# An embedding lookup with position add: instruction streams and semaphores written by hand, stores in four interleaved transfers

## The chip, the cores and the metric

The kernel runs on one core of a Trainium2 chip. The metric is the device time of one execution in microseconds (us); of the kernel before, 10 runs gave a median of 184.74 us (184.63 to 184.87). The profile is of one further execution.

A core has five engines that run their own instruction streams[...]: PE (TensorE), DVE (VectorE), ACT (ScalarE), POOL (GpSimd) and SP (SyncE). Transfers between the chip's memory (HBM) and the on-chip memory (SBUF, 128 partitions) are made by 16 DMA engines, which SP and POOL feed by two different queues.

## The reference

```python
batch, seq_len, vocab_size, d_model = 32, 512, 50000, 512
# indices (32, 512) int32; embedding_table (50000, 512) float32; position_embed (512, 512) float32
token_embed = embedding_table[indices]
return (token_embed + position_embed).astype(np.float32)
```

For each of 32 x 512 tokens a row of 2 KB is fetched from the table, the row of its position is added, and the sum is written: 33.5 MB are read at scattered places and 33.5 MB are written.

## The kernel before

A sequence of 512 tokens is laid over 128 partitions with K = 4 tokens in each, so that partition p holds tokens 4p to 4p + 3; a sequence is a tile of 128 x 4 x 512 floats, 8 KB in a partition, 1 MB in all. One *gather* (an indirect DMA, line 88, issued from POOL) fetches column k of a sequence, one row for each partition, 256 KB. One *add* on DVE (line 94) adds the position rows of that column in place. A *store* (line 97, issued from SP) writes one, two or four columns to `out`.

Ahead of the loop over the 32 sequences SP loads the indices of the first sequence (`idx0`, line 49), all indices with a sequence in each partition (`idx_raw`, line 51) and the position rows (`pos_sb`, line 56). As a gather wants its indices one to a partition, `idx_raw` is turned: DVE converts it to float (line 68), PE transposes it in four steps against an identity that POOL made (lines 60 to 73), and DVE converts it back (line 75). ACT copies the position rows to PSUM (line 79), from where DVE adds them. The first sequence needs only `idx0`, so its gathers start before the turning is done.

The kernel is written for a framework that takes care of buffers and semaphores: it gives each tile a buffer of a pool (`data_pool`, BUFS = 20), puts the needed waits before each instruction, and has the engines run in the order of the source. Each gather and each store is counted by one of eight semaphores in turn; thus a gather also waits for the gather eight before it, and a store for the store eight before it. What one instruction cannot wait for by itself is put into wait-only instructions (EVENT_SEMAPHORE) in front of it. At the end SP waits for all these semaphores in ten such instructions (they carry the line of the launch, L132), and the engines meet in a barrier.

How a sequence is cut into stores is set by hand (lines 100 to 106): sequences 0, 1 and 31 in four stores of one column each (256 KB, 2 KB to a partition), sequences 2 to 5 and 30 in two stores of two columns (512 KB, 4 KB to a partition), all others in one store of 1 MB (8 KB to a partition). That makes 12 + 10 + 24 = 46 stores. Every store or part of a sequence has a buffer of its own.

## Time and profile before

| what | value |
|---|---|
| median of 10 runs | 184.74 us |
| the profiled execution's own time | 184.82 us |
| its span, from the first to the last instruction of the profile | 183.1 us |
| what lies around the span | 1.72 us |
| bytes moved | 68.33 MB, mean 373 GB/s |
| gathers: count, mean time of one on POOL | 128, 0.949 us |
| adds: count, mean time of one on DVE | 128, 0.688 us |
| stores: count, time of one on SP | 46, 0.332 us |
| first gather starts, last gather starts | 2.78 us, 162.12 us |
| last add ends | 172.43 us |
| last store issued | 173.88 us |
| last DMA packet ends | 174.35 us |

How to read it: the page gives each engine's busy time, and below it the span in 40 slices of 4.58 us with the busy tenths of each. The line DMA is the mean busy share of the 16 DMA engines. A group of instructions stands under its line of the kernel, with its operation, the tile that it writes and reads, and how often it occurs. An SPq row is an instruction that SP's queue carries out; it counts as no busy time. In the table by stage each row has the stretch, its length, the busy time and count of the five engines, the clock, the share of DMA and the GB/s. The packet records of the trace have the time, the size and the queue of each single packet: q0 carries the gathers, q1 what SP issues.

Lines 121 and 132 are lines of the launch: the start and the end that the framework puts around the kernel.

### The profile page before, as it was taken

The numbers are of one execution on the slowest core, as the hardware profiler recorded it, in microseconds if no ns is written. First come the engines' busy times: TensorE is split into PE (matmuls) and PEld (weight loads), VectorE is DVE, ScalarE is ACT, GpSimd is POOL, SyncE is SP. The second block draws the span as 40 slices with busy tenths as digits, with TensorE's granted clock in tenths as the row PEclk, the third lists the DMA queues.
The fourth block names the chain that finished last, engine by engine and source line by source line (L and its number), as shares of the span: only waits on it lengthen the run. The fifth ranks groups of instructions, "written<-read, shape, count | busy, mean of one in ns | idle before, by whom it ended". The sixth has DMA issues, their size and how long they took to land.

```text
span 183.1 us, 480 instructions
## 1 busy us (share of the span) xinstructions
PE 0.7 (0%) x4; PEld 0.6 (0%) x4; DVE 87.6 (48%) x130; ACT 3.6 (2%) x5; POOL 122.1 (67%) x134
## 2 busy tenths in 40 slices
PE   0000000000000000000000000000000000000000
PEld 0000000000000000000000000000000000000000
DVE  1253654555647444448255554544547464643300
ACT  3400000000000000000000000000000000000000
POOL 4777777777777777877877877777777777740000
DMA  4889999999999999999999999999999999999900
GB/s 137 311 248 375 388 397 375 407 384 408 392 402 412 411 398 419 405 419 401 414 409 413 418 413 417 406 424 408 414 418 415 422 409 419 408 415 417 372 6 0
DMA packets 17635, 68.33 MB, mean 373 GB/s; under 512 B 3008, under 2 KB 3008, under 8 KB 14560
## 3 DMA queue, kind: packets, MB, share of 16 engines
q0 software_dynamic: 10240, 33.56, 48.2%
q1 hardware_dynamic: 7392, 34.74, 46.3%
q14 instruction: 3, 0.02, 0.0%
HBM read 34.74 MB, written 33.55 MB: 373 GB/s over the span
## 4 chain that ended last, share of the span: by engine, by line
issue 58%; DMA 18%; POOL 8%; SPq 5%; DVE 3%; DVEq 1%; POOLq 1%
DMA data<-in_embedding_table_dram,idx_t 10%; POOL data L88 8%; DMA out_dram<-data 7%; SPq L97 5%; DVE data L94 3%; DMA idx<-in_indices_dram 1%; DVEq L94 1%; POOLq L88 1%
## 5 line engine op out<-in xcount | busy, mean ns | idle before, releaser
L88 POOL DMA_INDIRECT data<-in_embedding_table_dram,idx_t x124 | 117.6, 948 | 37.8 <-issue 37.2
L94 DVE TENSOR_TENSOR data<-data,pos_ps 128x512 f32<-128x512 f32 x128 | 86.7, 688 | 80.4 <-DMA data<-in_embedding_table_dram,idx_t 41.2
L88 POOL DMA_INDIRECT data<-in_embedding_table_dram,idx x4 | 4.0, 996 | 2.5 <-DMA idx<-in_indices_dram 1.6
L79 ACT COPY pos_ps<-pos_sb 128x512 f32<-128x512 f32 x4 | 2.4, 589 | 5.0 <-DMA pos_sb<-in_position_embed_dram 3.3
L68 DVE CAST idx_f<-idx_raw 32x512 f32<-32x512 int32 x1 | 0.6, 606 | 3.5 <-DMA idx_raw<-in_indices_dram 3.5
L79 ACT ACT_TABLE_LOAD x1 | 1.3, 1283 | 0.8 <-PEq L121 0.8
L75 DVE CAST idx_t<-turned 128x128 int32<-128x128 f32 x1 | 0.3, 292 | 0.8 <-PE turned L73 0.8
L73 PE MATMUL turned<-ident,idx_f 32*128 32x32 f32 x4 | 0.7, 301 | 4.3 <-DVE idx_f L68 4.3
L73 PEld LDWEIGHTS turned<-ident,idx_f 32*128 32x128 f32 x4 | 0.6, 208 | 4.2 <-issue 4.2
L121 POOL MEMSET const-float32-0.0<- 128x1 f32 x1 | 0.1, 104 | 0.3 <-issue 0.3
L60 POOL MEMSET ones<- 32x32 f32 x1 | 0.1, 115 | 0.3 <-POOLq L121 0.3
L62 POOL TENSOR_SCALAR_AFFINE_SELECT ident<-ones 32x32 f32<-32x32 f32 x1 | 0.2, 204 | 0.1
L121 POOL MEMSET const-uint8-127<- 128x1 uint8 x1 | 0.1, 121 | 0.0
L121 POOL MEMSET const-bfloat16-1.0<- 128x1 bf16 x1 | 0.1, 115 | 0.0
L121 POOL MEMSET const-float32-1.0<- 128x1 f32 x1 | 0.1, 107 | 0.0
## 6 DMA issues: line engine op xcount, KB each, us to landing
out_dram<-data SPq DMA_DIRECT2D x24, 1024.0 KB
out_dram<-data SPq DMA_DIRECT2D x10, 512.0 KB
out_dram<-data SPq DMA_DIRECT2D x12, 256.0 KB
data<-in_embedding_table_dram,idx_t POOLq DMA_INDIRECT x124
pos_sb<-in_position_embed_dram SPq DMA_DIRECT2D x4, 256.0 KB
idx_raw<-in_indices_dram SPq DMA_DIRECT2D x1, 128.0 KB
data<-in_embedding_table_dram,idx POOLq DMA_INDIRECT x4
idx<-in_indices_dram SPq DMA_DIRECT2D x1, 4.0 KB
```

Source lines behind the costliest of these rows:

```text
L60: nc.gpsimd.memset(ones[:], 1.0)
L62: nc.gpsimd.affine_select(out=ident[:], in_=ones[:], pattern=[[-1, B]], compare_op=mybir.AluOpType.is_equal, fill=0.0, base=0, channel_mul ...
L68: nc.vector.tensor_copy(out=idx_f[:].rearrange("b p k -> b (p k)"), in_=idx_raw[:, :, 0])
L73: nc.tensor.transpose(turned[:, k, :], idx_f[:, :, k], ident[:])
L75: nc.vector.tensor_copy(out=idx_t[:], in_=turned[:])
L79: nc.scalar.copy(out=pos_ps[k][:], in_=pos_sb[k][:])
L88: nc.gpsimd.indirect_dma_start(out=data[:, j, :], out_offset=None, in_=table, in_offset=bass.IndirectOffsetOnAxis(ap=where, axis=0),)
L94: nc.vector.tensor_tensor(out=data[:, j, :], in0=data[:, j, :], in1=pos_ps[k][:], op=add)
L97: nc.sync.dma_start(out=out_rows[b][:, at : at + n, :], in_=data[:])
L121: nc = _bacc.Bacc("TRN2", target_bir_lowering=False, num_devices=1)
```

## The change

The tiles are kept, and so are the loads, the turning of the indices, the gathers and the adds. What is new:

```diff
-    data_pool = ctx.enter_context(tc.tile_pool(name="data", bufs=BUFS))
+    slots = [sbuf(f"slot{n}", [P, K, D], f32) for n in range(SLOTS)]
...
+    stores = []
+    for b in range(B):
+        if b == 0 or b == B - 1:
+            split, combs = (1, 1, 1, 1), 1
+        elif b <= 2:
+            split, combs = (2, 2), 2
+        else:
+            split, combs = (K,), COMBS
+        at = 0
+        for n in split:
+            for j in range(combs):
+                adds = min(b * K + at + n + j, B * K)
+                stores.append((adds, b, at, n, j, combs))
+            at += n
+    stores.sort()
...
+    def rounds(g):
+        return 16 * (g // LANES + 1)
+
+    with tc.tile_critical():
...
+        nc.gpsimd.wait_ge(s_first, 16)
+        for g in range(B * K):
+            b, k = divmod(g, K)
+            if g == K:
+                nc.gpsimd.wait_ge(s_idx, 1)
+            if b >= SLOTS and k == 0:
+                done = sum(1 for x in stores if x[1] == b - SLOTS)
+                nc.gpsimd.wait_ge(s_out[b - SLOTS], 16 * done)
+            where = idx0[:, 2 * k : 2 * k + 1] if b == 0 else idx_t[:, k, b : b + 1]
+            ins = nc.gpsimd.indirect_dma_start(
+                out=slots[b % SLOTS][:, k, :],
...
+            ).then_inc(s_gather[g % LANES], 16)
+            if g >= LANES:
+                ins._wait_ge(s_gather[g % LANES], rounds(g - LANES))
...
+        for g in range(B * K):
+            b, k = divmod(g, K)
+            if b == 0:
+                nc.vector.wait_ge(s_ps, k + 1)
+            part = slots[b % SLOTS][:, k, :]
+            nc.vector.tensor_tensor(
+                out=part, in0=part, in1=pos_ps[k][:], op=add
+            )._wait_ge(s_gather[g % LANES], rounds(g)).then_inc(s_add, 1)
...
+        for adds, b, at, n, j, combs in stores:
+            done = s_out.get(b, s_rest)
+            rest += done is s_rest
+            nc.sync.dma_start(
+                out=out_rows[b][j::combs, at : at + n, :],
+                in_=slots[b % SLOTS][j::combs, at : at + n, :],
+            )._wait_ge(s_add, adds).then_inc(done, 16)
+        nc.sync.wait_ge(s_rest, 16 * rest)
```

## The prediction

> **What bounds the kernel now.** I read the page first: busy shares, then the forty slices and the DMA queues; then the table by stage, the rows of the gather and of the SP queue, and last the two ends. The page of the kernel before:

> ```profile
> PE 0.7 (0%) x4; PEld 0.6 (0%) x4; DVE 87.6 (48%) x130; ACT 3.6 (2%) x5; POOL 122.1 (67%) x134
> ...
> DMA  4889999999999999999999999999999999999900
> ...
> q0 software_dynamic: 10240, 33.56, 48.2%
> q1 hardware_dynamic: 7392, 34.74, 46.3%
> ```

> No engine is near 100%, but the sixteen DMA engines are: the two queues' packets took 48.2% + 46.3% of the span, and the digits are 9 from the fourth slice until the last two, which are 0. The table by stage, whose last two columns are the DMA share and GB/s:

> ```profile
> 2.00:10.00 8.00, 0.66 (x4) 0.55 (x4) 2.05 (x4) 2.45 (x5) 5.70 (x6) 1.00 0.85 282
> 10.00:20.00 10.00, 0.00 (x0) 0.00 (x0) 4.56 (x8) 0.00 (x0) 7.56 (x9) 1.00 0.96 325
> 20.00:40.00 20.00, 0.00 (x0) 0.00 (x0) 10.70 (x16) 0.00 (x0) 15.12 (x17) 1.00 1.03 393
> 40.00:163.00 123.00, 0.00 (x0) 0.00 (x0) 65.50 (x97) 0.00 (x0) 93.08 (x99) 1.00 1.02 411
> 163.00:171.00 8.00, 0.00 (x0) 0.00 (x0) 3.99 (x6) 0.00 (x0) 0.07 (x1) 1.00 1.02 418
> 171.00:175.00 4.00, 0.00 (x0) 0.00 (x0) 0.83 (x2) 0.00 (x0) 0.00 (x0) 1.00 0.69 265
> 175.00:183.10 8.10, 0.00 (x0) 0.00 (x0) 0.00 (x0) 0.00 (x0) 0.00 (x0) 1.00 0.00 0
> ```

> From 20 to 171 us DMA is full. From 175 to 183.1 us nothing moves and no engine computes: 8.1 us of pure ending. The rows of the gather (L88), of the stores (L97) and of the end (L132), with minimum/median/maximum ns:

> ```profile
> L88 POOL DMA_INDIRECT data<-in_embedding_table_dram,idx_t x124: 945/949/957, 8.0 to 162.1; - x124
> ...
> L97 SPq DMA_DIRECT2D out_dram<-data x46: 332/332/700, 8.8 to 173.9; - x46
> L97 SPq EVENT_SEMAPHORE  x44: 17/17/701, 10.6 to 172.5; - x44
> ...
> L132 SPq EVENT_SEMAPHORE  x11: 2/3/699, 175.3 to 182.5; - x11
> ```

> POOL starts a gather every (162.12 - 2.78) / 127 = 1.2547 us and is never held up. A gather of 262,144 bytes and its store ask for 524,288 / 1.2547 = 418 GB/s; DMA delivers 411. So POOL and DMA are almost level, and the gathers' queue falls behind slowly: the chain of waits shows 4.01 us from issue to landing at 8 us, 7.56 us at 88 us, and the last one takes about 9 us. What is new in the last row: ten of the eleven wait-only instructions lie between the last store and 182.28 us, and their starts are 0.7 or 1.4 us apart although the semaphores they name are filled (the last packet ended at 174.35, the last store's semaphore at 174.58). A wait on SP costs 17 ns before 170 us; from 170.1 us on, SP steps in units of 0.7 us.

> [...] in the packet records 256 KB stores ran at 84 ns for 2 KB, 1 MB stores at 309 ns for 8 KB, so row length made a difference of 8%, and transfer size none that I can see. [...] 832 4-byte packets on q1 are 52 x 16. [...] the one 32-partition transfer here (the block idx_raw, loaded beside pos_sb) had a median of 237 ns for a 4 KB packet, against 159 ns elsewhere.

> **The change part by part.** The sum is made on the profiled execution: 184.82 us, span 183.1, so 1.72 us lie around it; it stands 0.08 us above the median of 184.74.

> *Start.* The critical section puts two SP instructions (a no-op and a branch) ahead of the first load, and the other engines wait for them. Such steps are some 0.05 us apart here. All that follows moves: +0.15, bounds 0 and +0.5 us.

> *POOL.* Still 128 gathers of 0.949 + 0.305 us. The look-back goes from 8 gathers (10.0 us) to 16 (20 us), the buffers from 20 to 24, one for each sequence; neither wait held POOL before, as its starts are even throughout. Gain 0. It would matter if landing came to exceed 10 us, and is now a cover of 11 us. The new waits for a slot stand before gathers 96, 100 and so on, with later gathers behind them; they are for stores about 20 sequences old. Cost 0; the cover is some 100 us.

> *DVE, ACT, PE.* The same 128 adds of 0.688 us, with one wait in each and four extra for pos_ps, which is ready as before. DVE is busy at 48%, so nothing.

> *SP issue.* 46 stores become 128, but 44 wait instructions go. 128 x (0.332 + 0.05) = 49 us, spread over 165: one issue for each 1.25 us add, at the end two for each of adds 125 to 127, 0.76 us. Hidden while SP is at its fast step; at the slow step, two records of 0.7 us, a store would take 1.4 us and no longer keep up with an add.

> *DMA work.* 82 more stores x 9 ns for one increment packet in each engine = +0.74 us. 1 MB goes from 2 KB to 8 KB packets: 128 x (4 x 84 - 309) / 16 = -0.22 us; 3 MB from 4 KB: 384 x (2 x 159 - 309) / 16 = -0.22 us. Sum +0.30 us, all on the path, as DMA is full. The packet time itself, 309 ns for 8 KB, is the unknown: finer mixing of stores and gathers could take away the gathers' excess (165.7 ns on average against 159: 6.7 x 64 packets x 128 gathers / 16 = 3.4 us)[...]. I take 309 and keep -3 and +9 for the range.

> *Order of the stores.* Quarter j of a sequence waits for j more adds, so its stores trail by up to three adds, 0.75 MB. The stores behind it in SP's queue wait for later adds anyway. Near 10 to 20 us, where the DMA share is only 0.96, this opens a hole: +0.5 (0 to +1.8, all 0.75 MB at 411 GB/s). At the end it fills one: from 171 to 175 DMA moved 265 x 4 = 1.06 MB, which at 411 takes 2.6 us, so 1.4 us stood empty around the last adds and SP's slow last issue; with half a megabyte of stores still queued I take 1.0 of it back.

> DMA then ends at 174.35 + 0.15 + 0.30 + 0.5 - 1.0 = 174.30.

> *End.* Ten wait-only instructions that check 19 semaphores become one wait for s_rest, then six short instructions and a round among the engines. Before, this took 182.29 - 174.35 = 7.94 us. At the fast step: 0.25 us until the last semaphore (174.34 to 174.58 before), 7 x 0.05, and one round of 0.4 us (two final rounds took 182.34 to 183.10), together 1.0 us. Then the final rounds and rest, 0.82 us as before. 174.30 + 1.0 + 0.82 + 1.72 = 177.84; with half of one slow step of 0.7 us on top, 178.2. At the slow step the seven cost 4.9 us, and if each leaves two records, 9.8.

> **The rivals.** *A, the end goes fast* (178.2): fewer waits, all data already landed. For it: SP ran at 17 ns for 170 us with this kind of instruction. Its doubt: I don't know why SP slows down; if it is the place in the stream (after some 95 instructions), the slow stretch falls among stores near the middle and is hidden.

> *B, the slow step stays at the end* (181.7): it starts at about 170 us whatever the instruction. Seven steps at 0.7 us instead of 0.05: +4.6 us, and the last seven stores take 1.4 us instead of 0.38, of which the DMA's rest hides most; the 1.0 us taken back at the end and part of the tail go: 178.2 + 4.6 = 182.8 with single steps throughout, less about 1.1 us since some steps pair up (the last three before ended within 0.02 us). For it: in the trace it is tied to nothing but the time and SP's own stream.

> *C, slower* (187.4): [...] 28 sequences x 4 transfers x 2 packets in each engine = 224 packets. At 350 ns instead of 309 they cost 224 x 0.041 = 9.2 us, on a path that is full: 178.2 + 9.2 = 187.4. It decides from (184.82 - 178.2) / 224 = 30 ns, thus from 339 ns on. For it: idx_raw's slow packets. Against: [...] idx_raw was a block loaded beside others.

> *D, no change*: A's gain eaten by a mild C or by B at two records for each step; a narrow window of 0.7 us.

> **How the numbers follow.** A 0.44, B 0.30, C 0.23, D 0.03. The likeliest is A, so 178.2; its own range is 176.6 to 179.8. The lower end is A with part of the 3.4 us of excess gone; the upper, 187.5, takes in B (up to 184.4) and the nearer half of C. A measurement here can tell about 0.2%, 0.37 us, from no change: faster 0.74, same 0.03, slower 0.23.

> **What would show it.** Right: no run of 0.7 us waits behind the last store, and the zero slices at the end shrink from 8.1 us to about 2; DMA near 411 GB/s between 40 and 163 us; gathers still 1.255 us apart; 8 KB packets at 309 ns. B shows as SP instructions 0.7 us apart after 170 us, C as 8 KB packets above 339 ns and fewer GB/s in the middle. The hole would show as less than 325 GB/s between 10 and 20 us. The prediction fails outright if POOL's cadence changes, or if the slow step comes so early that the stores fall behind the adds.

## The result, and the profile after

The changed kernel takes 195.95 us (195.04 to 196.51, 8 runs) against 184.73 (184.56 to 184.90, 28 runs) for the kernel before on the same chip: ratio 1.060, 95% interval 1.0588 to 1.0611. It is slower by 11.2 us, and outside the range of the prediction. The profiled execution took 196.55 us with a span of 194.8. The experiments ran on five chips, on three of which the kernel before takes 184.5 to 184.9 us and on two 178.2; so each ratio below is against the kernel before on the same chip, and times are compared only where the chip is the same or the text says otherwise.

From the page of the changed kernel:

```profile
PE 0.7 (0%) x4; PEld 0.6 (0%) x4; DVE 88.1 (45%) x130; ACT 3.6 (2%) x5; POOL 122.1 (63%) x134
...
DMA  4989999999999999999999999999999999835460
...
q0 software_dynamic: 10240, 33.56, 47.0%
q1 hardware_dynamic: 7936, 34.75, 43.7%
```

POOL and DVE did the same work as before (122.1 us, and 88.1 against 87.6). The last six digits of the DMA row, 999900 before, are now 835460. The end is no longer empty; for some 20 us, in four slices, it is about half full. The table by stage (stretch, its length, busy time and count of the five engines, clock, DMA share, GB/s):

```profile
2.00:10.00 8.00, 0.68 (x4) 0.55 (x4) 1.89 (x4) 2.63 (x5) 5.45 (x6) 1.00 0.83 271
10.00:20.00 10.00, 0.00 (x0) 0.00 (x0) 4.56 (x8) 0.00 (x0) 7.56 (x9) 1.00 0.94 318
20.00:40.00 20.00, 0.00 (x0) 0.00 (x0) 10.62 (x16) 0.00 (x0) 15.12 (x17) 1.00 1.00 369
40.00:163.00 123.00, 0.00 (x0) 0.00 (x0) 67.35 (x99) 0.00 (x0) 93.13 (x99) 1.00 1.01 398
163.00:171.00 8.00, 0.00 (x0) 0.00 (x0) 3.66 (x6) 0.00 (x0) 0.30 (x1) 1.00 0.83 342
171.00:180.00 9.00, 0.00 (x0) 0.00 (x0) 0.00 (x0) 0.00 (x0) 0.00 (x0) 1.00 0.46 189
180.00:190.00 10.00, 0.00 (x0) 0.00 (x0) 0.00 (x0) 0.00 (x0) 0.00 (x0) 1.00 0.53 211
190.00:194.80 4.80, 0.00 (x0) 0.00 (x0) 0.00 (x0) 0.00 (x0) 0.00 (x0) 1.00 0.07 25
```

The last add ends at 170.3 us, two microseconds earlier than before. After it no engine computes, yet DMA moves 189 to 211 GB/s until 190.46 us: stores that could have gone long ago. Who holds them back? The rows of the gather (L125) and of the store on SP's queue (L167) say it, with minimum/median/maximum ns; the first two lines are from the whole span, the last two are the store's row in two windows, 8 to 47 us and 52 to 184 us:

```profile
L125 POOL DMA_INDIRECT slot<-in_embedding_table_dram,idx_t x124: 945/949/959, 8.2 to 162.4; - x124
...
L167 SPq DMA_DIRECT2D out_dram<-slot x128: 3/700/1559, 9.5 to 188.8; - x128
...
L167 SPq DMA_DIRECT2D out_dram<-slot x26: 332/472/1559, 9.5 to 45.9; - x26
L167 SPq DMA_DIRECT2D out_dram<-slot x91: 5/700/1480, 52.5 to 183.0; - x91
```

The gathers are untouched. A store takes SP 0.47 us (the median) until about 46 us and 0.70 us from 51 us on, mostly with another 0.70 to 0.76 us of gap before the next: (183.0 - 52.5) / 90 = 1.45 us from store to store, while the adds that release them come every 1.255 us. This is the slow step that the kernel before showed only at its end. SP falls behind by 0.2 us for each store, and 98 stores later it is 18 us late. 262,144 bytes in 1.455 us are 180 GB/s, close to the 189 of the stretch from 171 to 180 us.

The second thing to see is behind the last store, in the rows of the critical section's own exit (L98):

```profile
L98 SPq NOP  x2: 18/18/18, 0.8 to 193.8; - x2
...
L98 POOLq DRAIN  x1: 2515/2515/2515, 191.2 to 191.2; - x1
```

SP has seen all stores at 191.0 us, then waits for POOL, whose drain takes 2.515 us, and only then executes its NOP at 193.8.

### The profile page after: what moved, and what is told of

It reads as the page before. It is cut to its first block, busy times and chain, and to the rows that moved or that the text cites. A ratio compares the mean times of both kernels' runs of the same rounds, so it can differ in the third digit from the quotient of the medians.

```text
span 194.8 us, 480 instructions
## 1 busy us (share of the span) xinstructions
PE 0.7 (0%) x4; PEld 0.6 (0%) x4; DVE 88.1 (45%) x130; ACT 3.6 (2%) x5; POOL 122.1 (63%) x134
## 3 DMA queue, kind: packets, MB, share of 16 engines
q0 software_dynamic: 10240, 33.56, 47.0%
HBM read 34.74 MB, written 33.55 MB: 351 GB/s over the span
## 4 chain that ended last, share of the span: by engine, by line
POOL 56%; issue 23%; DMA 5%; DVE 4%; SPq 0%; POOLq 0%
POOL slot L125 56%; DMA slot<-in_embedding_table_dram,idx_t 4%; DVE slot L154 4%; DMA idx<-in_indices_dram 1%; SPq L197 0%; SPq L98 0%; POOLq L123 0%
## 5 line engine op out<-in xcount | busy, mean ns | idle before, releaser
L125 POOL DMA_INDIRECT slot<-in_embedding_table_dram,idx_t x124 | 117.6, 948 | 37.8 <-issue 37.8
L154 DVE TENSOR_TENSOR slot<-slot,pos_ps 128x512 f32<-128x512 f32 x128 | 87.2, 688 | 77.6 <-issue 58.6
L125 POOL DMA_INDIRECT slot<-in_embedding_table_dram,idx x4 | 4.0, 997 | 2.5 <-DMA idx<-in_indices_dram 1.6
```

What stands on the lines that cost most here:

```text
L125: ins = nc.gpsimd.indirect_dma_start(out=slots[b % SLOTS][:, k, :], out_offset=None, in_=table, in_offset=bass.IndirectOffsetOnAxis(ap=whe ...
L154: nc.vector.tensor_tensor(out=part, in0=part, in1=pos_ps[k][:], op=add)._wait_ge(s_gather[g % LANES], rounds(g)).then_inc(s_add, 1)
```

## The experiments

The questions were four: is it SP's slow step or the shape of the stores; what brings the slow step on; what does the hand-written exit cost; and is there anything left of the hoped-for gain. "SP slow" below means instructions of 0.7 or 1.4 us, or gaps of that size with nothing to wait for.

**Shape and queue of the stores** (before: 184.51 us). The first kernel stores full sequences whole, 44 stores instead of 128:

```diff
-COMBS = 4
+COMBS = 1
```

> The changed kernel with COMBS = 1: sequences 3 to 30 each in one store of 1 MB, so 44 stores in place of 128, all else kept. Theory S (SP falls into a step of 0.7 us, a store then takes 1.455 us, longer than the 1.255 us between two gathers, and the stores pile up): with one store in 5 us SP's issue can't be late, DMA ends near 174 us and the whole takes 177 to 183 us, depending on whether the step reaches the end. Theory R (what costs is the new order and the hand-written waits: stores that trail the adds, waits that hold POOL or DVE): little changes, 190 us or more. Theory T (transfers of 32 partitions are slow in the DMA engines): also under 184, but then the 8 KB packets of the changed kernel would have been longer than 309 ns, and they were 311.

Measured 184.42 us, ratio 0.9993 (0.9986 to 1.0000). From the table by stage:

```profile
40.00:163.00 123.00, 0.00 (x0) 0.00 (x0) 65.29 (x97) 0.00 (x0) 92.94 (x99) 1.00 1.02 413
```

SP stays fast until all data is out (413 GB/s, last packet at 174.98), and turns slow at 176.0 us, after three fast instructions of the exit. So the hand-written streams by themselves are neither the loss nor a gain here: the slow step is back where it was before, at the end, and the time misses the 177 to 183 us that were expected.

The second keeps the 128 stores and gives every other one to ACT:

```diff
+        for i, (adds, b, at, n, j, combs) in enumerate(stores):
+            queue = nc.scalar if i % 2 else nc.sync
```

> The changed kernel with every second store issued from ACT, whose stream is idle after 6 us. Same transfers, same order, same waits. Theory S: each of the two queues has one store in 2.5 us, under the 1.455 us of the slow step, so stores keep up with the adds even if both slow down: 177 to 184 us. Theories R and T: the transfers and their order are the same, so 194 to 197 us as in the changed kernel.

188.40 us, ratio 1.0231 (1.0191 to 1.0270). The rows of the stores:

```profile
L168 SPq DMA_DIRECT2D out_dram<-slot x64: 332/468/577, 9.2 to 171.1; - x64
L168 ACTq DMA_DIRECT2D out_dram<-slot x64: 339/476/548, 10.3 to 172.6; - x64
```

The stores keep up (413 GB/s; SP has seen all of them land at 175.34 us, at 191.0 in the changed kernel), neither engine is slow before the end, and SP is slow from 176.05 to 187.26 us, all through the exit. That exit is why the time lies above the expected 177 to 184 us. The third keeps one store for each add, but as a column of all 128 partitions (2 KB rows), and not as a *comb*, a store that takes every fourth partition:

```diff
-        if b == 0 or b == B - 1:
-            split, combs = (1, 1, 1, 1), 1
...
+        split, combs = (1, 1, 1, 1), 1
```

> The changed kernel with all 32 sequences cut by columns, 128 partitions and 2 KB in each, four stores for a sequence, so again 128 stores of 256 KB and one for each add, but none waits for a later add and none takes every fourth partition. Theory S: the number of SP's instructions is the same, so SP slows down and the stores pile up: 192 to 200 us; the 2 KB packets add 28 x 128 x (4 x 84 - 309) / 16 = 6 us to the DMA work where that is the limit. Theories R (trailing) and T (32 partitions): fast, 178 to 186 us.

186.99 us, ratio 1.0120 (1.0100 to 1.0139). The store's row between 56 and 180 us:

```profile
L162 SPq DMA_DIRECT2D out_dram<-slot x89: 5/700/1395, 55.5 to 178.7; - x89
```

SP is slow here too, from 54 us on; so it isn't the comb. But a store costs (178.7 - 55.5) / 88 = 1.40 us instead of 1.45, and the last one goes at 181.5 instead of 188.8. So 195.95 - 186.99, about 9 of the 11 us lost, come with the comb (two chips, on which the kernel before differs by 0.2 us), and not by its packets (311 ns for 8 KB, as before; their median is 309 in both). Where they come from is in part an estimate: under the slow step a store costs 0.05 us more, which makes some 5 us for 98 of them, and the combs start further behind the adds (30 stores were out at 51.1 us, here 34 at 51.4), which makes another 4 times 1.4 us. The time is below the expected 192 to 200 us for the same two reasons. The fourth is the 44-store version with three wait-only instructions ahead of each 1 MB store, for a semaphore filled long before (six waits in the source; the build puts two into one instruction):

```diff
+            if combs == 1 and n == K:
+                for _ in range(6):
+                    nc.sync.wait_ge(s_first, 16)
```

> The kernel of whole stores (COMBS = 1) with three instructions ahead of each 1 MB store that only wait for a semaphore filled at the start: SP has as many instructions as the changed kernel, but 44 stores. If the slow step comes from the number of instructions that SP has carried out (theory S1), SP slows down in the middle; as four instructions of up to 1.4 us fit into the 5 us of a sequence only just, the time is 182 to 192 us. If it comes from the number or kind of the DMAs it issues (theory S2), the waits take 17 ns and the time is that of the kernel of whole stores within 0.5 us.

187.25 us, ratio 1.0138 (1.0121 to 1.0154). The fillers' row, before and after 30 us:

```profile
L169 SPq EVENT_SEMAPHORE  x5: 28/28/176, 25.1 to 29.6; - x5
L169 SPq EVENT_SEMAPHORE  x79: 5/700/1397, 30.3 to 175.9; - x79
```

With 44 stores, but four SP instructions for each sequence, the slow step is there from 30.3 us. What counts is the number of SP's instructions, not the number of its DMAs.

**Stores from ACT** (another chip; before: 178.16 us, and in the four traces SP shows no slow step). The first two replace `nc.sync.dma_start` of the store by `nc.scalar.dma_start` in the 44-store version and in the changed kernel, the third does the same in the kernel before, and the fourth is the changed kernel with two combs for four:

```diff
-COMBS = 4
+COMBS = 2
```

> The kernel of whole stores (COMBS = 1) with all 44 stores issued from ACT; SP keeps the six loads and the end. Theory S2 (the slow step belongs to SP and grows out of the work that SP has done): SP has done almost nothing, so its end runs at the fast step; data done at about 175.3, then 0.3 us, 2.5 us for POOL's drain and 0.7 us of rounds, so 180 to 181 us. Theory E (the slow step is tied to the end of a run, whatever SP did): 184 to 185 us as with the stores on SP. Should ACT fall into the slow step in SP's place, it shows as ACT instructions 0.7 us apart.

> The changed kernel with all 128 stores issued from ACT in place of SP. If the slow step is SP's alone, ACT issues each store in 0.48 us and keeps up with the adds: 180 to 185 us. If any engine that issues a store in every 1.25 us falls into the step, ACT does, and the time is 194 to 197 us as in the changed kernel.

> The kernel before with its 46 stores issued from ACT, nothing else. SP then has six loads and the ten waits of the end. Theory S2: the ten waits take some 0.05 us each in place of 0.7, and the last two stores are not held up by 1.4 us: 176.5 to 178.5 us. Theory E: the end is as before, 183.5 to 185 us.

> The changed kernel with COMBS = 2: sequences 3 to 30 in two stores of every second partition, 72 stores on SP, one in 2.5 us. If the slow step comes from the number of instructions SP has carried out (about 40 in the changed kernel), SP slows down in the middle too, but a store of 1.455 us still keeps up, and the time is 182 to 186 us. If it comes from how close they follow each other, SP stays fast until the end: 182 to 185 us. The two differ in the trace: SP instructions 0.7 us apart from 60 us on, or only after 165 us.

Measured 180.68, 181.27, 177.69 and 181.85 us; ratios 1.0144 (1.0109 to 1.0179), 1.0177 (1.0139 to 1.0215), 0.9981 (0.9959 to 1.0003) and 1.0225 (1.0185 to 1.0266). The second is the changed kernel with its stores free of SP:

```profile
L167 ACTq DMA_DIRECT2D out_dram<-slot x128: 338/476/1002, 8.8 to 171.7; - x128
...
40.00:163.00 123.00, 0.00 (x0) 0.00 (x0) 66.31 (x97) 0.00 (x0) 93.14 (x99) 1.00 1.02 413
```

All stores keep up and data ends at 175.55 us, 14.9 us before that of the changed kernel. But this chip can't tell that ACT is the cure, as SP isn't slow on it either, with 72 stores of its own (median 0.472 us); that the first three times lie in the expected ranges is no test of it. What the runs do show is that the second still loses 1.8%, and the version with 72 stores on a fast SP 2.2%: without any slow step the change doesn't gain either. In all three hand-written versions POOL's drain takes 2.5 us at the exit; in the kernel before POOL drains from about 160 to 172 us, beside the last adds.

**The exit, and both kernels again** (before: 184.90 us). The changed kernel and the kernel before unaltered; then the changed kernel with one line behind POOL's last gather, so that POOL drains beside the last adds; then that line in the 44-store version with stores on ACT:

```diff
+        nc.gpsimd.drain()
```

> The changed kernel once more, unaltered, beside the kernel before. Theory S (SP's step of 0.7 us belongs to the place where the kernel runs, and costs the change time only where it comes while stores are left): if the kernel before takes about 184.6 us here, 195 to 196.5 us, SP at 1.40 to 1.46 us per store from some point on; if it takes about 178.2 us, SP steps at 0.05 us throughout, a store takes 0.48 us, stores keep up with the adds, and what is left is the exit: 181.3 us (ratio 1.015 to 1.02), with a gap of about 2.3 us ahead of SP's no-op while POOL drains. Rival (the store pattern itself brings the slow step, wherever it runs): 195 us in either case.

> The kernel before, unaltered, with a trace from the same chip as the others of this set: ratio 1.00. Theory S: if it takes about 178.2 us, no SP instruction takes 0.7 us and the ten wait-only instructions at the end are over within 0.5 us of the last store's semaphore; if about 184.6 us, they are 0.7 or 1.4 us apart as in the first profile.

> The changed kernel with one drain on POOL directly after its last gather, so that POOL's 2.5 us of draining run beside the last adds and stores and not behind the last store. Theory E (POOL's drain is serial in the exit): 2.0 to 2.4 us less than the unaltered changed kernel of the same set, and the drain at the exit takes under 0.1 us. Rival (the drain at the exit takes its 2.5 us whatever was drained before, or waits for the stores): no difference, within 0.3 us.

> Hand-written streams with the full sequences in one store of 1 MB (44 stores), all stores issued from ACT, and the drain on POOL after the last gather. Theories S and E together: nothing is left for a slow SP to hold up but the exit's handful of steps. If the kernel before takes about 178.2 us here: 180.7 - 2.3 = 178.4 us, ratio 0.995 to 1.005. If it takes about 184.6 us: stores end near 175.4, then eight or nine SP steps of 0.7 to 1.4 us, 182 to 185 us. Rival to E: 180.7 us, ratio 1.014.

196.26, 184.96, 193.74 and 184.61 us; ratios 1.0605 (1.0577 to 1.0632), 1.0001 (0.9992 to 1.0010), 1.0468 (1.0444 to 1.0492) and 0.9980 (0.9970 to 0.9991). The drain at the exit of the third:

```profile
L98 POOLq DRAIN  x1: 41/41/41, 190.6 to 190.6; - x1
```

41 ns instead of 2,515: the early drain is worth 196.26 - 193.74 = 2.5 us. The changed kernel repeats its loss on this second chip, with SP slow from 47 us on, and the kernel before its slow end. The fourth has SP idle for 171 us, and then its exit at 175.5 goes fast for three instructions and slow to 183.5 us. A long rest does not keep SP fast for the ten short instructions of an exit.

**What brings the slow step on.** For every run I counted SP's instructions and took off one for each 1.40 us that passed, never below zero; what remains is the *excess*. In the runs up to and with the second pause probe below, ten of eleven onsets after 40 us came at an excess of 3.2 to 3.9, as if SP had a *stock* of about three instructions that may come faster (the last expectation of this group has nine, which is one short). The eleventh was 7.3, at 54 us; two earlier ones, at 30 and 39.6 us, were 7.4 and 10.7. And early in a run the rule doesn't hold. These are the stores of the kernel before and their waits from 8 to 40 us:

```profile
L97 SPq DMA_DIRECT2D out_dram<-data x16: 332/332/348, 8.8 to 39.5; - x16
L97 SPq EVENT_SEMAPHORE  x15: 17/17/17, 10.6 to 39.9; - x15
```

That is one instruction per us, 1.0 against 0.714, and an excess of 6.5 to 10.6 from 13 to 49 us, without a slow step. So early on SP has more in hand than three; why is not known. (Single stores of 0.73 to 1.56 us between 20 and 36 us are not counted as the slow step: on the chip without it SP's and ACT's stores took up to 0.93 and 1.00 us there.) The rule was read off afterwards, so it had to forecast something. The probes start from the 44-store version with stores on ACT and the early drain, and let SP execute wait-only instructions that hold nobody up:

```diff
+        for g in range(B * K):
+            nc.sync.wait_ge(s_add, g + 1)
+            nc.sync.wait_ge(s_add, g + 1)
```

> The version with 44 stores on ACT and the early drain, whose SP now also executes one wait-only instruction for each add (128, 0.797 per us), which nothing waits for until the end. Theory R (SP's slow step comes once it has had more than one instruction per 1.40 us for a while, whatever they are): SP turns slow at 45 to 60 us, as with 128 stores, then takes 1.4 us per wait and is through with them at 176 to 182 us; the time grows by at most 5 us, for nothing else hangs on SP. Rival M (it needs DMA issues among SP's instructions): all waits take under 0.05 us beyond their semaphore until the last add at about 171 us. Where the kernel before takes about 178.2 us, no slow step in any case, and the run tells nothing on R.

> As the one before, but SP executes these waits only for adds 1 to 24 and 65 to 128, with a pause from about 40 to 90 us. Theory R with a stock that the pause fills: slow from some 25 to 45 waits after the pause, at 120 to 145 us. Rival T (what counts is the time: from about 50 us on, any instruction that follows within 1.4 us is slow): slow within three waits of the pause, at 90 to 95 us.

> As the first probe, but SP executes three waits for four adds: 0.60 per us, below one per 1.40 us (0.714). Theory R: never slow before the end at about 172 us. Rival T: slow from about 50 us on where two waits stand 1.25 us apart.

These three ran where the kernel before takes 178.15 us. No SP instruction was slow, so they tell nothing of the rule: 179.28, 178.93 and 179.28 us, ratios 1.0057 (1.0030 to 1.0084), 1.0044 (1.0019 to 1.0069), 1.0055 (1.0038 to 1.0072). They do show that hand-written streams with an early drain, and with the waits of the probe, still lose half a per cent there. Also the waits did not run as written: put by the build into pairs, the first one ended only at 93 us in the first probe, and then two instructions came for each add.

The next has a pause in the waits, and ran where the kernel before takes 184.88 us:

```diff
+            if g < 64 or g >= 96:
+                nc.sync.wait_ge(s_add, g + 1)
+                nc.sync.wait_ge(s_add, g + 1)
```

> As the probe with a pause, but SP executes its waits for adds 1 to 64, pauses for adds 65 to 96 (about 85 to 128 us), and goes on for adds 97 to 128; stores are on ACT. Meant for a run where the kernel before takes about 184.6 us (where it takes 178.2, it tells nothing). Theory R: slow from 45 to 60 us on, at 1.4 us per wait; after the pause fast again for at least ten waits. Rival M (it needs DMA issues on SP): fast until the end. Rival T (the time counts): fast or slow at first, slow within three waits after the pause.

187.17 us (one run). The waits (two lines, L174 and L175) again began late, at 72 us. L174 in the windows 72 to 75.5, 76 to 112, 130 to 135.6 and 135.6 to 176 us:

```profile
L174 SPq EVENT_SEMAPHORE  x2: 28/28/28, 74.2 to 75.2; - x2
L174 SPq EVENT_SEMAPHORE  x13: 5/700/1395, 76.2 to 110.5; - x13
L174 SPq EVENT_SEMAPHORE  x3: 28/28/28, 132.4 to 135.5; - x3
L174 SPq EVENT_SEMAPHORE  x14: 5/700/1387, 137.8 to 174.2; - x14
```

Wait-only instructions with no DMA of SP's own among them turn slow, so DMA issues are not needed. After the pause five waits are fast, not ten as I had expected, and then it is slow again: a small stock refills, and the time in the run doesn't decide. The last probe puts the stock's size to the test, with bursts on either side of it:

```diff
+        for b in range(8, B - 1):
+            for n in range(3 if b < 20 else 5):
+                nc.sync.nop()._wait_ge(s_add, (b + 1) * K).then_inc(s_tick, 1)
```

> The version with 44 stores on ACT and the early drain; SP executes, besides, wait-only instructions in bursts, one burst after the last add of a sequence: three for each of sequences 8 to 19, five for each of sequences 20 to 30. Theory R with its stock, as read from the runs so far (nine of eleven onsets after 40 us came when SP had executed 3.2 to 3.9 instructions more than one per 1.40 us): no slow step before sequence 20, at about 114 us; then the fourth or fifth instruction of the first burst of five takes 0.7 or 1.4 us, and so in the bursts after it. Rival Q (only a rate that lasts counts, with a stock above ten): no slow step before 160 us. Rival T (the time counts): slow from the first burst, at about 52 us. Where the kernel before takes about 178.2 us, no slow step, and the run tells nothing.

186.15 us (one run; before 184.58). The bursts' row in the windows 40 to 114, 114 to 120 and 120 to 184 us:

```profile
L174 SPq EVENT_SEMAPHORE  x36: 17/17/133, 54.3 to 111.1; - x36
L174 SPq EVENT_SEMAPHORE  x5: 17/168/709, 115.4 to 117.8; - x5
L174 SPq EVENT_SEMAPHORE  x50: 2/700/1396, 121.1 to 182.9; - x50
```

Twelve bursts of three: all fast, for 57 us. The first burst of five, from the trace (start us, took ns):

```
115.363   17
115.429   17
115.496  168
116.365  701
117.765  709
```

The fourth is slow, at an excess of 3.3, as forecast from a stock of about three. The rivals, a lasting rate alone and the time, are out for this stage of a run, as far as one run shows.

**The best version.** The kernel before with its stores on ACT, on a chip where the kernel before takes 184.58 us:

```diff
-            nc.sync.dma_start(out=out_rows[b][:, at : at + n, :], in_=data[:])
+            nc.scalar.dma_start(out=out_rows[b][:, at : at + n, :], in_=data[:])
```

> The kernel before with all its stores issued from ACT, and nothing else changed. Theory R with its stock: where the kernel before takes about 184.6 us, SP comes to its ten wait-only instructions at the end with its stock full, so three of them are fast and the other seven and the short ones after them go at 0.7 to 1.4 us: 182 to 184.5 us, ratio 0.985 to 0.999, as the last stores are no longer issued at the slow step. Rival (the end is the same, since the waits at the end take what they took): 184.6 us, ratio 1.00. Where the kernel before takes about 178.2 us: 177.7 us, ratio 0.997 to 1.000 as in the first run of this version.

183.88 us, ratio 0.9961 (0.9947 to 0.9975). SP's waits at the end start at 170.2 us, five are fast while they wait for real, and the slow step comes at 175.6, at an excess of 3.1. On the other kind of chip it was 0.9981, with an interval that takes in 1, so no gain is shown there. It lost on neither, and the change is one word.

## Why the prediction was wrong

The measured 196.55 us of the profiled execution lie 18.35 above 178.2. In the prediction's own steps:

*SP issue* is the step that failed, with 14.9 us: data ended at 190.46, and at 175.55 in the same program with the stores on ACT. These are two chips, but with every other store on ACT, on a chip with the slow step, all stores had landed by 175.34. The prediction priced it rightly: "at the slow step, two records of 0.7 us, a store would take 1.4 us and no longer keep up with an add". It then took "Hidden while SP is at its fast step" for the case. Its case A even hoped that a slow stretch "falls among stores near the middle and is hidden", although that step had shown that it can't be. What was missing is when the step comes. It was not place in the stream (instruction 96 before, 40 after, 58 and 29 in two experiments) and not the time; after the first 50 us it is rate. SP is then good for one instruction per 1.40 us, 0.714 per us, and about three on top (an excess of 3.2 to 3.9 at ten of eleven onsets). Before: two for each sequence of 5.02 us, 0.40 per us, until the smaller stores of the end, with a wait each, came 1.8 us apart (four steps from 163.88 to 171.16 us), 1.1 per us. Changed: one for each add, 0.797 per us. Both numbers stood in the prediction ("one issue for each 1.25 us add" and 1.4 us); that the first would bring on the second was not seen. Merging each wait into its store, which saved 44 instructions, could not make up for 82 stores more. The fast price was low as well: 0.332 us is that of a store of 128 partitions, one of 32 takes 0.468, which would still have been hidden.

*End* was too low by 2.2 us: 4.38 us from the last packet to the end of the span against 1.0 + 0.82 and the half step. This is the drain of POOL (2.515 us). The prediction counted SP's short instructions and "one round of 0.4 us", but not what each engine does in that round. SP's own steps were fast there, because the slow stretch had just ended.

*Order of the stores* and *DMA work*: without the slow step data ended at 175.55, not 174.30, and 1.28 us after that of the kernel before with stores on ACT (174.28, same chip). The 44-store version ended at 174.82. So hand-written streams cost 0.54 us and combs 0.73 us in the data, where the steps summed to -0.05. These are single profiles, and the runs of each version spread by 0.8 to 1.9 us, so the size isn't shown. The hole that was expected at 10 to 20 us stands rather at 20 to 40: 390 GB/s there in the kernel before with its stores on ACT, 379 with 44 stores and 376 with 128. In *DMA work* the sum was right, though not its parts: one sequence goes from 2 KB to 4 KB rows and four from 4 KB to 8 KB, which makes 0.43 us in place of 0.44.

*Start* (+0.15; the gathers moved from 2.78 to 3.03 us: +0.25), *POOL* (1.2545 us between gathers, no waits), *DVE, ACT, PE*, and the packet time (311 ns for 8 KB, taken as 309) held. So case C, packets of 339 ns and more in the stores of 32 partitions, is out. The gathers' 4 KB packets were no faster either: between 40 and 160 us 171.9 ns on average beside slow stores against 165.8 before (162.9 on the other chip with the stores on ACT).

Case B had the right cause in the wrong place: it let the slow step begin at about 170 us, which gave 181.7. The prediction's last sentence names what happened, "the slow step comes so early that the stores fall behind the adds", but gave it no chance.

What the slow step is stays open: no run shows what holds SP. A store of the changed kernel and a wait of the second pause probe took it alike, at a median of 0.70 us. Nor is it known why two of five chips show no slow step, and what ends it early (at 182.3 us in one run, 188.8 in another, with instructions still waiting).

## What to carry to other kernels

Count the instructions on each engine that issues DMAs, for the stage that matters, and hold the rate against what the trace shows at its worst, not at its usual: 17 ns and 332 ns were the fast prices of an engine that could also take 1.40 us. Where an engine shows a slow price in one place, find the rate there and ask whether the change brings that rate elsewhere. Here the time in which SP issues a store was the bound (1.45 us for a store whose data takes 0.64 us at 411 GB/s), and with every other store on ACT the stores kept up.

## What the hardware showed unexpectedly

On three of five chips SP executes one instruction per 1.40 us for long, with a stock of about three after the first 50 us (excess 3.2 to 3.9 at ten of eleven onsets) and of more before (an excess of up to 10.6). ACT with 128 stores showed none of it on a chip where SP was fast (median 0.476 us, at most 1.00), and with 64 none where SP was slow at its end (at most 0.548 us); 128 stores from ACT on such a chip were not tried. The drain of POOL takes 2.515 us when it first comes 12 to 28 us after POOL's last gather, and 0.041 us when another drain came before. A store of 32 partitions x 8 KB takes 0.468 us to issue, one of 128 partitions 0.332 us.
